# Second layer's experts: the first product as three products of 192 columns into one result

## The chip, the cores and the metric

The kernel runs on one core of a Trainium2 chip, as one program. A core has a matrix engine (TensorE, PE in the rows), a vector engine (VectorE, DVE), a scalar engine (ScalarE, ACT), GpSimd (POOL), and SyncE (SP), which issues most loads. TensorE's weight loads have rows of their own (PEld). The metric is the device time of one execution in microseconds, the median over several. Times within an execution come from one that was recorded by the hardware profiler.

## The reference

The model is two blocks, one after the other, each of two layers, on 256 tokens of width 1024. The change is in the expert part (`peer`) of the first block's second layer. Each token picks 16 of 16384 experts for each of 8 heads; an expert is a row u and a row v of two tables:

```
q = (xc @ wq).reshape(C, PEER_HEADS, 2, PEER_KEY_DIM)
...
top, pos = lax.top_k(cand, PEER_TOPK)
eidx = jnp.take_along_axis(cidx, pos, axis=-1)
g = jax.nn.softmax(top, axis=-1).astype(xc.dtype)
a = jax.nn.gelu(jnp.einsum('chkd,cd->chk', u_tab[eidx], xc))
return jnp.einsum('chk,chkd->cd', g * a, v_tab[eidx])
```

## The kernel before

Instead of gathering the rows of the picked experts for each token, the kernel computes most tokens densely: the 16384 experts are 128 blocks of 128, and for each block the first product multiplies the block's u rows with the tokens, gelu follows, the values are multiplied with a matrix of routing weights that is zero where an expert wasn't picked, and the second product multiplies with the block's v rows. In the second layer there are 256 tokens; `DENSE` gives 192 of them (TD = 192) to this dense way, and the other 64 go by gathers: an indirect DMA on GpSimd fetches rows (`gathered`, lines 892 to 909), and VectorE makes two passes of 1024 columns over each (line 895 takes the dot product, line 909 adds to a sum what the gather before it gave).

Float32 is multiplied as three products of two halves. `split` (lines 127 and 128) makes a high half on ScalarE and a low half on VectorE in a type that TensorE multiplies in one pass. `mm3` (lines 182 to 187) multiplies high by high (line 185), high by low (186) and low by high (187) and adds all three in one result bank; its first operand is the stationary one, which TensorE loads as weights. Weights come through `wload`: a DMA on SyncE's queue into `raw`, `split` into `whi` and `wlo`, four of each ahead.

`peer` (from line 697) calls `expert_in` for each block. Blocks 0 to 29 of the second layer take the branch `whole` ahead of the loop. The other 98 blocks run within the loop over c, in each round with: the first product of block c; gelu into `G` (line 868); the product with the routing weights into `A` (line 790); its split into `Ahl` (line 793, and line 795 for the last 64 tokens apart); up to one gather; and the second product of the block three rounds earlier (LAG = 3). The second product is six 512 wide products by `mm3` for 128 tokens and four of line 823 for the remaining 64.

The first product goes over the width of 1024 in eight slices of 128 (k). For TD = 192 the high and the low half of the tokens lie side by side in `h2`, so one product 384 wide (line 859) multiplies the high half of the weights with both at once: columns 0 to 191 of the bank get high by high, columns 192 to 383 high by low. A second product, 192 wide (line 858, or 861 in the first slice), adds low by high to columns 0 to 191. After the last slice ScalarE copies the right part out of the bank (line 864) and VectorE adds the left part to it (line 865), and gelu reads the sum.

The program is written in the order above, and a scheduler of the framework puts the instructions of each engine in an order of its own. Each engine works through its own in that order, and semaphores tie them together.

Of the kernel before, what the change touches and what calls it, by code (L numbers as in the profile page):

```python
# [9 lines left out]
F32 = mybir.dt.float32  # L10
# [33 lines left out]
def r3(ap, a):  # L44
    return ap.rearrange("p (a b) -> p a b", a=a)


class Net:
# [791 lines left out]

    def expert_in(self, lp, l, c, h2, h32, TD, whole):


        nc, mm = self.nc, self.nc.tensor.matmul
        ps = self.psum(True)
        src = ps[:, :TD]
        if whole:
            u = r3(self.wraw(self.i["peer_uT"][l, c]), 8)
            for k in range(8):
                mm(src, u[:, k], h32[:, k, :TD], start=k == 0, stop=k == 7)  # L850
        else:
            u = self.wload(self.i["peer_uT"][l, c], 8)
            for k in range(8):
                if TD > 192:
                    self.mm3(src, (u[0][:, k], u[1][:, k]), (h2[:, k, 0, :TD], h2[:, k, 1, :TD]), k == 0, k == 7)
                    continue
                if k:
                    mm(src, u[1][:, k], h2[:, k, 0, :TD], start=False, stop=False)  # L858
                self.last = mm(r3(ps[:, :2 * TD], 2), u[0][:, k], h2[:, k, :, :TD], start=k == 0, stop=k == 7).ins  # L859
                if k == 0:  # L860
                    mm(src, u[1][:, k], h2[:, k, 0, :TD], start=False, stop=False)
            if TD <= 192:
                both = lp.tile([128, TD], F32, tag="Gs", name="Gs", bufs=2)
                nc.scalar.copy(both, ps[:, TD:2 * TD])
                nc.vector.tensor_add(both, both, src)
                src = both
        g = lp.tile([128, TD], F32, tag="G", name="G", bufs=15 if TD > 256 else 36)
        nc.scalar.activation(g, src, AF.Gelu_apprx_tanh)
        return g
# [766 lines left out]
```

## Time and profile before

| what | us |
|---|---|
| median of 3 runs | 3451.87 |
| lowest and highest run | 3449.92, 3456.09 |
| the profiled execution | 3459.74 |
| span of its instructions | 3458.0 |
| TensorE busy in the span | 3322.4 (96%) |
| VectorE busy | 2624.0 (76%) |
| ScalarE busy | 1777.2 (51%) |

The span runs from the first to the last instruction of the profiled execution; its own time is 1.74 us longer. TensorE's products are pipelined: one starts before the one ahead of it has ended, so that their durations add up to more than the time that passes, and distances between starts say more.

### The profile page before, as it was taken

To read this page: it belongs to the slowest core of one execution; us is meant where nothing else is said; L and a number is where in the kernel's file an instruction comes from. 1 tells how busy PE (TensorE), PEld (TensorE's weight loads), DVE (VectorE), ACT (ScalarE), POOL (GpSimd) and SP (SyncE) were. 2 spreads that over 40 slices of the span, in tenths; PEclk is the share of its full clock that TensorE was granted. 3 is DMA by queue.
4 is the path that set the end of the run, shared out by engine and by line. 5 is a ranking of instruction groups with operands and counts; after the bars stand their busy time and mean duration, and the time that the engine had idled before them with its cause. 6 is when DMAs were issued, how large, how long until landed. Compare 5 with 4: busy or idle time off the path is not lost.

```text
span 3458.0 us, 53681 instructions
## 1 busy us (share of the span) xinstructions
PE 3322.4 (96%) x19573; PEld 2856.2 (83%) x19573; DVE 2624.0 (76%) x5467; ACT 1777.2 (51%) x3763; POOL 513.2 (15%) x434
## 2 busy tenths in 40 slices
PE   8999999899899999999999999989999989999998
PEld 5665788788888888888877988869999988889887
DVE  3533449988988888999966679599999957746764
ACT  3433332396444444444445545557777745545554
POOL 0000000112333333333300000122222100000000
PEclk9999999999999999999999999999999999999999
DMA  7555232457999999999944555799999843255332
GB/s 254 179 201 209 84 125 88 163 175 287 375 385 370 369 384 369 385 394 390 381 176 153 176 169 172 264 346 382 373 378 372 327 159 137 98 180 180 120 122 104
DMA packets 196456, 860.56 MB, mean 249 GB/s; under 512 B 23920, under 2 KB 25664, under 8 KB 159712
## 3 DMA queue, kind: packets, MB, share of 16 engines
q1 hardware_dynamic: 141840, 505.94, 40.4%
q0 software_dynamic: 54352, 351.20, 26.5%
q8 instruction: 154, 2.52, 0.3%
q14 instruction: 110, 0.90, 0.1%
HBM read 816.15 MB, written 40.89 MB: 248 GB/s over the span
## 4 chain that ended last, share of the span: by engine, by line
PE 54%; issue 24%; DVE 9%; DMA 7%; POOL 5%; ACT 1%; POOLq 0%; DVEq 0%; SPq 0%; ACTq 0%
PE pf L187 6%; PE pf L186 6%; PE pf L185 6%; PE ps L185 5%; PE ps L187 5%; PE ps L186 5%; PE pf L859 4%; POOL gat L892 3%; DMA gat<-peer_uv,idx 3%; PE ps L823 3%; DVE wlo L128 3%; PE pf L858 2%; DVE gacc L909 2%; PE pf L369 2%; PE ps L261 1%
## 5 line engine op out<-in xcount | busy, mean ns | idle before, releaser
L128 DVE TENSOR_TENSOR wlo<-raw,whi 128x1024 fp32r<-128x1024 f32 x778 | 940.9, 1221 | 386.4 <-ACT whi L127 381.5
L127 ACT CAST whi<-raw 128x1024 fp32r<-128x1024 f32 x778 | 814.4, 1047 | 574.4 <-PE pf L186 206.6
L892 POOL DMA_INDIRECT gat<-peer_uv,idx x256 | 403.9, 1578 | 926.0 <-DVE gacc L909 895.0
L187 PE MATMUL pf<-h2hl,wlo 128*128 128x320 f32 (+2 forms) x1152 | 373.2, 324 | 43.3 <-DVE wlo L128 43.1
L895 DVE SCALAR_TENSOR_TENSOR gat<-gat,h 128x1024 f32<-128x1024 f32 x256 | 311.9, 1219 | 77.4 <-DMA gat<-peer_uv,idx 77.1
L185 PE MATMUL pf<-h2hl,whi 128*128 128x320 f32 (+2 forms) x1152 | 370.3, 321 | 0.0
L186 PE MATMUL pf<-h2hl,whi 128*128 128x320 f32 (+2 forms) x1152 | 369.7, 321 | 0.0
L909 DVE SCALAR_TENSOR_TENSOR gacc<-gat,pga,gacc 128x1024 f32<-128x1024 f32 x253 | 323.4, 1278 | 0.0
L186 PE MATMUL ps<-wlo,Ahl 128*128 128x512 f32 x768 | 302.2, 393 | 7.0 <-DVE wlo L128 7.0
L185 PE MATMUL ps<-whi,Ahl 128*128 128x512 f32 x768 | 301.1, 396 | 2.5 <-ACT Ahl L127 2.5
L187 PE MATMUL ps<-whi,Ahl 128*128 128x512 f32 x768 | 301.3, 392 | 0.5 <-DVE Ahl L128 0.5
L187 PEld LDWEIGHTS pf<-h2hl,wlo 128*128 128x128 f32 x1152 | 223.3, 194 | 52.1 <-DVE wlo L128 49.4
L859 PE MATMUL pf<-h2hl,whi 128*128 128x384 f32 x784 | 238.9, 360 | 3.9 <-ACT whi L127 3.7
L185 PEld LDWEIGHTS pf<-h2hl,whi 128*128 128x128 f32 x1152 | 223.2, 194 | 7.4
L186 PEld LDWEIGHTS pf<-h2hl,whi 128*128 128x128 f32 x1152 | 222.6, 193 | 7.4
L127 ACT CAST Ahl<-A 128x320 fp32r<-128x320 f32 (+1 forms) x256 | 103.7, 405 | 220.7 <-DVE A L790 215.8
L1021 PE MATMUL ps<-o,og 128*128 128x128 f32 x1024 | 171.1, 297 | 6.0 <-ACT og L1020 4.8
L858 PE MATMUL pf<-h2hl,wlo 128*128 128x192 f32 x686 | 175.3, 256 | 0.0
L187 PEld LDWEIGHTS ps<-whi,Ahl 128*128 128x128 f32 x768 | 144.7, 188 | 33.5 <-DVE Ahl L128 1.0
L186 PEld LDWEIGHTS ps<-wlo,Ahl 128*128 128x128 f32 x768 | 144.6, 188 | 32.0 <-DVE wlo L128 9.7
L896 ACT ACTIVATE pga<-pga 128x1 f32<-128x1 f32 x256 | 51.4, 201 | 230.3 <-DVE gat L895 230.2
L185 PEld LDWEIGHTS ps<-whi,Ahl 128*128 128x128 f32 x768 | 144.8, 189 | 26.8 <-ACT Ahl L127 4.5
(591 smaller groups left out, 7749.4 us busy)
## 6 DMA issues: line engine op xcount, KB each, us to landing
raw<-peer_uT SPq DMA_DIRECT2D x256, 512.0 KB, 7.2
raw<-peer_v SPq DMA_DIRECT2D x256, 512.0 KB, 7.1
raw<-ada_w SPq DMA_DIRECT2D x96, 512.0 KB, 4.6
wd<-wb POOLq DMA_DIRECT2D x32, 1024.0 KB, 6.4
raw<-w_g SPq DMA_DIRECT2D x48, 512.0 KB, 3.8
win<-wd POOLq DMA_DIRECT2D x16, 1280.0 KB, 11.0
raw<-wq SPq DMA_DIRECT2D x32, 512.0 KB, 3.6
raw<-w2o SPq DMA_DIRECT2D x32, 512.0 KB, 3.2
```

The source lines that it names most:

```text
L127: nc.scalar.copy(hi, src)
L128: nc.vector.tensor_sub(lo, src, hi.bitcast(F32))
L185: mm(ps, ah, bh, start=start, stop=False)
L186: mm(ps, ah, bl, start=False, stop=False)
L187: self.last = mm(ps, al, bh, start=False, stop=stop).ins
L823: nc.tensor.matmul(acc[nd][n], ahl[:, 2 * TD - part:], v[e][:, n], start=b == 0 and e == 0, stop=b == 127 and e == 1)
L858: mm(src, u[1][:, k], h2[:, k, 0, :TD], start=False, stop=False)
L859: self.last = mm(r3(ps[:, :2 * TD], 2), u[0][:, k], h2[:, k, :, :TD], start=k == 0, stop=k == 7).ins
L892: nc.gpsimd.indirect_dma_start(out=uv.rearrange("p a b -> p (a b)"), out_offset=None, in_=i["peer_uv"], in_offset=bass.IndirectOffsetOnAxi ...
L895: nc.vector.scalar_tensor_tensor(uv[:, 0], uv[:, 0], 1.0, h2, op0=OP.mult, op1=OP.mult, accum_out=a[:, 0:1])
L909: self.nc.vector.scalar_tensor_tensor(acc, uv[:, 1], a[:, 1:2], acc, op0=OP.mult, op1=OP.add)
L1021: nc.tensor.matmul(ps[:, j * 128:j * 128 + 128], og[:, j], o1[:, jj], start=True, stop=True)
```

## The change

For TD = 192 the first product now goes through `mm3` as it does in the first layer: in each slice three products of 192 columns, high by high, high by low and low by high, all added in columns 0 to 191 of the bank. The copy on ScalarE, the addition on VectorE and their buffer `Gs` are gone; gelu reads the bank.

```
-                if TD > 192:
-                    self.mm3(src, (u[0][:, k], u[1][:, k]), (h2[:, k, 0, :TD], h2[:, k, 1, :TD]), k == 0, k == 7)
-                    continue
-                if k:
-                    mm(src, u[1][:, k], h2[:, k, 0, :TD], start=False, stop=False)
-                self.last = mm(r3(ps[:, :2 * TD], 2), u[0][:, k], h2[:, k, :, :TD], start=k == 0, stop=k == 7).ins
-                if k == 0:
-                    mm(src, u[1][:, k], h2[:, k, 0, :TD], start=False, stop=False)
-            if TD <= 192:
-                both = lp.tile([128, TD], F32, tag="Gs", name="Gs", bufs=2)
-                nc.scalar.copy(both, ps[:, TD:2 * TD])
-                nc.vector.tensor_add(both, both, src)
-                src = both
+                self.mm3(src, (u[0][:, k], u[1][:, k]), (h2[:, k, 0, :TD], h2[:, k, 1, :TD]), k == 0, k == 7)
```

In the following rows an instruction has its line, its operation, what it writes and reads, and its size; `pf` and `ps` are result banks, `u` comes as `whi` and `wlo`. Lines behind the edit have numbers lower by 13 in the changed kernel.

TensorE in a round of the loop, before, from the last instruction of a second product on into the first product of a block (its first two slices):

```order
L823 MATMUL ps<-wlo,Ahl 128x512
L859 MATMUL pf<-h2hl,whi 128x384
L861 MATMUL pf<-h2hl,wlo 128x192
L858 MATMUL pf<-h2hl,wlo 128x192
L859 MATMUL pf<-h2hl,whi 128x384
L858 MATMUL pf<-h2hl,wlo 128x192
```

The same place in the changed kernel, its first slice and the start of the second:

```order
L823 MATMUL ps<-wlo,Ahl 128x512
L185 MATMUL pf<-h2hl,whi 128x192
L186 MATMUL pf<-h2hl,whi 128x192
L187 MATMUL pf<-h2hl,wlo 128x192
L185 MATMUL pf<-h2hl,whi 128x192
```

Sixteen instructions of a first product have become 24; the alternation with the second product of another block is the same in both.

VectorE in a round with a gather, before (`gat` is the gathered row, `gacc` the sum, `wlo` the low half of weights):

```order
L790 TENSOR_TENSOR A<-G,win 128x192
L895 SCALAR_TENSOR_TENSOR gat,pga<-gat,h_21336 128x1024
L128 TENSOR_TENSOR Ahl<-A,Ahl 128x192
L909 SCALAR_TENSOR_TENSOR gacc<-gat,pga,gacc 128x1024
L128 TENSOR_TENSOR wlo<-raw,whi 128x1024
L865 TENSOR_TENSOR Gs<-Gs,pf 128x192
L128 TENSOR_TENSOR wlo<-raw,whi 128x1024
```

And in the changed kernel:

```order
L790 TENSOR_TENSOR A<-G,win 128x192
L882 SCALAR_TENSOR_TENSOR gat,pga<-gat,h_21336 128x1024
L896 SCALAR_TENSOR_TENSOR gacc<-gat,pga,gacc 128x1024
L128 TENSOR_TENSOR Ahl<-A,Ahl 128x192
L128 TENSOR_TENSOR wlo<-raw,whi 128x1024 x2
```

The addition into `Gs` is gone, and the low half of `Ahl` has moved behind the second pass of the gather.

TensorE at the end of the stage, before: behind the last second product come products of another part (line 315), and then the fold that joins dense and gathered tokens (lines 833 and 834):

```order
L823 MATMUL ps<-wlo,Ahl 128x512
L315 MATMUL pf<-raw 128x128 x13
L833 MATMUL ps<-gat,fold 128x512
L834 MATMUL ps<-gacc,fold 128x512
L833 MATMUL ps<-gat,fold 128x512
L834 MATMUL ps<-gacc,fold 128x512
L315 MATMUL pf<-raw 128x128 x3
```

And in the changed kernel:

```order
L823 MATMUL ps<-wlo,Ahl 128x512
L833 MATMUL ps<-gat,fold 128x512
L834 MATMUL ps<-gacc,fold 128x512
L833 MATMUL ps<-gat,fold 128x512
L834 MATMUL ps<-gacc,fold 128x512
L315 MATMUL pf<-raw 128x128 x16
```

The 13 products have moved behind the fold.

## Rows read from the trace of the kernel before

**Rows 1.** Spans and granted clock of the core.

```profile
core 0: 3458.0 us, clock 0.986
```

**Rows 2.** Instructions of line 859: durations (min/median/max), first and last start.

```profile
L859 PE MATMUL pf<-h2hl,whi x784: 333/361/575, 2301.7 to 2764.9; 128*128 128x384 f32 x196
```

**Rows 3.** Busy time by stretch: length, engines with instruction counts, clock, DMA share, GB/s.

```profile
2700.00:2750.00 50.00, 50.00 (x285) 45.48 (x285) 47.44 (x73) 35.97 (x79) 6.69 (x4) 1.00 0.90 354
...
2310.00:2765.00 455.00, 453.36 (x2559) 412.02 (x2560) 435.79 (x655) 322.97 (x697) 90.17 (x62) 1.00 0.93 366
```

**Rows 4.** Chain that ended last, 2410 to 2480: shares, then start, length, what.

```profile
by line: PE pf L859 33.6%; PE ps L823 21.1%; PE pf L858 13.9%; PE ps L187 10.0%; PE ps L186 9.9%; PE ps L185 9.9%; PE pf L861 1.9%
...
2410.18 0.92 PE ps L823 x4
...
2479.18 0.92 PE ps L823 x4
```

**Rows 5.** Who waited for whom, 2310 to 2765: us in total, times, longest.

```profile
PE pf L859 <- ACT whi L127: 3.7, 1, 3.7
...
PE pf L859 <- DVE Gs L865: 0.2, 1, 0.2
```

**Rows 6.** Timeline of TensorE, one block's first product: start, length, what.

```profile
2502.95 0.33 PE L859 MATMUL pf<-h2hl,whi 128*128 128x384 f32 x1
2503.12 0.25 PE L861 MATMUL pf<-h2hl,wlo 128*128 128x192 f32 x1
2503.20 0.28 PE L858 MATMUL pf<-h2hl,wlo 128*128 128x192 f32 x1
2503.32 0.36 PE L859 MATMUL pf<-h2hl,whi 128*128 128x384 f32 x1
2503.51 0.25 PE L858 MATMUL pf<-h2hl,wlo 128*128 128x192 f32 x1
2503.60 0.37 PE L859 MATMUL pf<-h2hl,whi 128*128 128x384 f32 x1
2503.80 0.25 PE L858 MATMUL pf<-h2hl,wlo 128*128 128x192 f32 x1
...
2505.25 0.39 PE L185 MATMUL ps<-whi,Ahl 128*128 128x512 f32 x1
```

**Rows 7.** Timeline of TensorE's weight loads in the same block.

```profile
2503.12 0.19 PEld L858 LDWEIGHTS pf<-h2hl,wlo 128*128 128x128 f32 x1
2503.23 0.19 PEld L859 LDWEIGHTS pf<-h2hl,whi 128*128 128x128 f32 x1
2503.34 0.19 PEld L858 LDWEIGHTS pf<-h2hl,wlo 128*128 128x128 f32 x1
2503.51 0.19 PEld L859 LDWEIGHTS pf<-h2hl,whi 128*128 128x128 f32 x1
```

**Rows 8.** Timeline of line 1374, products 64 wide, and of its loads.

```profile
2912.12 1.95 PE L1374 MATMUL ps<-xs,dec 128*128 128x64 f32 x16
...
2912.07 1.86 PEld L1374 LDWEIGHTS ps<-xs,dec 128*128 128x128 f32 x16
...
L1374 PE MATMUL ps<-xs,dec x128: 275/275/323, 2912.1 to 3288.3; 128*128 128x64 f32 x128
```

**Rows 9.** Timeline of 256 wide products in the second layer's queries.

```profile
2059.56 0.28 PE L186 MATMUL pf<-h2hl,whi 128*128 128x256 f32 x1
...
2060.39 0.28 PE L187 MATMUL pf<-h2hl,wlo 128*128 128x256 f32 x1
```

**Rows 10.** Groups by line, 2310 to 2765: count, busy us, mean ns, idle before.

```profile
L865 DVE TENSOR_TENSOR Gs<-Gs,pf 128x192 f32<-128x192 f32 x97 | 33.6, 347 | 0.0
L864 ACT COPY Gs<-pf 128x192 f32<-128x192 f32 x97 | 30.5, 314 | 16.4 <-PE pf L859 13.6
```

**Rows 11.** Chain that ended last, behind the stage.

```profile
2778.11 2.90 PE pf L315 x26
```

**Rows 12.** Groups by line, whole span: loads of high halves in lines 185, 186.

```profile
L185 PEld LDWEIGHTS pf<-h2hl,whi 128*128 128x128 f32 x1152 | 223.2, 194 | 7.4
L186 PEld LDWEIGHTS pf<-h2hl,whi 128*128 128x128 f32 x1152 | 222.6, 193 | 7.4
```

## The prediction

> **What bounds the kernel now.** The execution spans 3458.0 us at a granted TensorE clock of 0.986 of full speed [rows 1]. The edit touches one stage only, and its own line finds it: the 384 wide products of line 859 run from 2301.7 to 2764.9 us, 784 of them [rows 2], which is 98 blocks by 8 slices. So the next view to read is the busy time of that stretch [rows 3]: TensorE is busy 453.36 of 455 us, VectorE 435.79, ScalarE 322.97, and the DMA engines stand at 0.93. Three resources are nearly full, so the shares alone don't say which one paces. The chain of waits does: in 70 us from the middle of the stage it names TensorE lines and nothing else, and the group of four closing products of a block returns every 4.60 us (2410.18 to 2479.18 is 69.00 us for 15 blocks) [rows 4]. The list of who waited for whom agrees: in the whole stage TensorE's products waited once for ScalarE, 3.7 us, and once for VectorE, 0.2 us [rows 5]. TensorE bounds the stage. Every nanosecond added to a block there comes out at the end, and relief on VectorE or ScalarE is worth nothing.
>
> **What a block costs on TensorE now.** The durations of single products overlap, so I go by the distances between starts [rows 6]. The first product of a block runs from 2502.95 to 2505.25, where the first of the 512 wide products starts: 2.30 us for 16 instructions. The other 2.30 us of 4.60 are ten 512 wide products, which the edit leaves alone. Within a slice there are about 0.09 us from a 192 wide product to the next one (2503.51 to 2503.60) and 0.20 us from a 384 wide one (2503.60 to 2503.80), together 0.29.
>
> **The change part by part.** Columns first: a slice streamed 384 + 192 = 576 columns and will stream 3 x 192 = 576. Columns neither gain nor lose anything. What is added is one product per slice, and with it one weight load: 24 of each per block instead of 16.
>
> The added load decides. At the start of a block the trace has several loads in a row with only 192 wide products between them, and these start at 2503.12, 2503.23, 2503.34: 0.11 us apart [rows 7], though a product of 192 columns needs only 0.08 to 0.09 (2503.12 to 2503.20). The products follow their loads: from the one at 2503.20 to the next it is 0.12 us, not 0.09 [rows 6]. In the rest of the block each 192 wide product alternates with a 384 wide one, which gives the loads time. A second place shows the same for a still narrower product: 16 products of 64 columns with full 128 x 128 float32 weights take 1.95 us, the last one's 0.275 among it, so (1.95 - 0.275)/15 = 0.112 us each, and their 16 loads (1.86 - 0.19)/15 = 0.111 us each [rows 8]. A third of the width, and the same distance: it isn't the columns. I read 0.108 to 0.112 us as the least distance of two loads of such weights. After the change every product is 192 wide, so every one waits for its load.
>
> The Trainium skill's page "TensorE: Matmul & The Clock Gate", section "LDWEIGHTS (loading the stationary operand)", gives a load as its columns divided by 1.2 per ns, so 107 ns for 128 columns, whatever matmul stands behind it. The rows above agree within a few ns; by the page alone a block's first product would be 24 x 107 ns = 2.57 us and the loss about 26 us (an estimate).
>
> By the rows, the first product of a block becomes 24 x 0.110 = 2.64 us against 2.30: plus 0.34 us. Lower bound within this case: 0.108, and the second product of a block, whose load starts early, 0.02 sooner: 2.57, plus 0.27. Upper bound: 0.112, so 2.69, plus 0.39. From above there is a further row: 256 wide products of the same kind, back to back, stand (2060.39 - 2059.56)/7 = 0.119 us apart [rows 9], and 192 wide ones should not be slower: 24 x 0.119 = 2.86, plus 0.56. From below, if the loads hide fully: 24 x 0.088 = 2.11, minus 0.19. I take 0.110, since rows 7 are these very weights at this very width.
>
> How many blocks pay: the first of the 98 waits for its weights [rows 5], the others for TensorE alone. 97 x 0.34 = **33 us**.
>
> What goes: ScalarE's copy of 128 x 192 out of the result (0.314 us) and VectorE's addition (0.347 us), once a block each [rows 10]. Neither is on the chain. VectorE's 435.79 us over 455/4.60 = 99 blocks are 4.40 us per block and fall to 4.06, while a block grows to 4.94: VectorE, 0.2 us from pacing the stage before, ends 0.9 us behind. The gelu reads the result directly, and its value is used three blocks later, so an earlier or later gelu costs nothing. VectorE's order within a block shifts: the low half of A now comes behind both passes of a gather. The accumulating pass takes the gather before, so it adds no wait, and three blocks of lead (15 us) hide the later low half; I cost it at nothing. Without that lead one pass more would stand ahead of the second kind of product in each block that has a gather. The DMA engines move the same bytes, 0.93 x 4.60 = 4.3 us per block, at a lower density. Behind the stage, 13 products that stood ahead of the final fold move behind it; 26 such instructions take 2.90 us [rows 11], so at most 1.5 us less before the fold, or as much later. I take nothing.
>
> **Sum.** The profiled execution took 3459.74 us, 7.87 above the median of the runs shown, 3451.87. With 33 us it would be 3492.7; against the median it is 3451.87 + 33 = **3484.9 us**, 1% slower.
>
> **The rivals.**
> *The loads hide: faster.* If a load can start under two products, all of them follow each other at 0.088 us, as those behind a 192 wide one do now; a block is 2.11 + 2.30 = 4.41 us, VectorE (4.06) and the DMA engines (4.3) still fit under it, and the stage gains 97 x 0.19 = 18 us: 3433 us. For it speak the distances of 0.08 and 0.09 in rows 6. Against it: each of those has a load that started under a longer product or right after one, and where three loads follow each other they are 0.11 apart [rows 7]. The two sides meet at 2.30/24 = 0.096 us per product. The Trainium skill's same page, section "Back-to-back issue gap", speaks for this side: it has 81 ns per matmul at 128 columns and 131 at 512 in a stream of loads and matmuls, so about 89 at 192 (an estimate), which would make some 3436 us. Here ten 512 wide products take 2.30 us, 230 ns each, so its figures don't fit this trace, and I give them little.
> *The load isn't added.* The first two products of a slice use the same weights. Were the second load left out, a slice had two loads (0.22 us) under 3 x 0.088 = 0.26 us, and 3433 us again. Against it: in the first layer's blocks the same helper makes the same pair of products, and both of its lines have 1152 loads [rows 12].
> *Slower still.* If what holds the 256 wide products at 0.119 is the load with something around it, and not their columns, a block costs 2.86 + 2.30 us: 97 x 0.56 = 54 us, 3506 us. The starts in rows 7 speak against it.
> *No difference.* That takes 0.093 to 0.099 us per product, within 0.2% (6.9 us) of 3451.87. No row shows such a distance.
>
> **How the numbers follow.** The load-paced case, 0.105 to 0.114 us, has 0.76; the 256 wide distance and beyond, 0.08; loads partly hidden, 0.099 to 0.105 and still slower, 0.05; no difference 0.03; the gain in both forms 0.08. A measurement of this kernel can tell about 0.2% from no change, so slower has 0.89, same 0.03, faster 0.08. The load-paced case with its bounds (26 to 38 us) and the spread of the runs shown (2 below, 4 above) is 3476 to 3494. To take in the case above it and a part of the partly hidden one, the range goes from 3472 to 3505.
>
> **What would show it.** The closing group of a block should return every 4.9 to 5.0 us, the loads of a block should start 0.11 us apart all through, TensorE should still be the whole chain of the stage, and VectorE's share there should fall from 96% to about 82%. Products 0.09 apart would prove the first rival, 0.12 the third. If the block takes 4.94 us and the total grows by much less than 33 us, the step from block to end failed and the time was made up behind the stage. Waits of TensorE for VectorE would say that the shifted order there was not free.

## The result, and the profile after

The changed kernel takes 3486.82 us in the median of 4 runs (3483.08 to 3492.55), the kernel before 3450.89 in 4. The ratio is 1.0106 with a 95% interval of 1.0089 to 1.0124: slower, by 35.9 us, where 33 were forecast.

The chain of waits in the same 70 us as [rows 4], changed kernel (shares of the stretch by line, then start, length, what):

```profile
by line: PE ps L823 18.4%; PE pf L187 18.2%; PE pf L186 18.0%; PE pf L185 17.5%; PE ps L185 9.7%; PE ps L186 9.3%; PE ps L187 9.2%
...
2412.70 0.91 PE ps L823 x4
...
2477.48 0.92 PE ps L823 x4
```

It names nothing but TensorE again, and the closing group returns 13 times in 64.78 us: 4.98 us a block instead of 4.60.

The busy time of the whole stage, which is now longer, answers [rows 3]:

```profile
2310.00:2800.00 490.00, 487.96 (x3321) 445.37 (x3320) 406.94 (x551) 292.30 (x594) 104.89 (x65) 1.00 0.88 337
```

TensorE is as full as before, 487.96 of 490 us. VectorE falls from 96% to 83%, the DMA engines from 0.93 to 0.88.

The timeline of TensorE in one block answers [rows 6]:

```profile
2503.15 0.25 PE L185 MATMUL pf<-h2hl,whi 128*128 128x192 f32 x1
2503.23 0.28 PE L186 MATMUL pf<-h2hl,whi 128*128 128x192 f32 x1
2503.35 0.28 PE L187 MATMUL pf<-h2hl,wlo 128*128 128x192 f32 x1
2503.46 0.27 PE L185 MATMUL pf<-h2hl,whi 128*128 128x192 f32 x1
...
2505.69 0.27 PE L187 MATMUL pf<-h2hl,wlo 128*128 128x192 f32 x1
2505.80 0.42 PE L185 MATMUL ps<-whi,Ahl 128*128 128x512 f32 x1
2506.07 0.40 PE L186 MATMUL ps<-wlo,Ahl 128*128 128x512 f32 x1
```

Only the first distance is 0.08; from there the products stand 0.11 to 0.12 apart, and the first product of the block lasts 2505.80 - 2503.15 = 2.65 us against 2.30. The first 512 wide product behind it takes 0.27 us to its successor, not the 0.23 of the other nine. The weight loads of the same block answer [rows 7]:

```profile
2503.15 0.19 PEld L186 LDWEIGHTS pf<-h2hl,whi 128*128 128x128 f32 x1
2503.26 0.19 PEld L187 LDWEIGHTS pf<-h2hl,wlo 128*128 128x128 f32 x1
2503.37 0.19 PEld L185 LDWEIGHTS pf<-h2hl,whi 128*128 128x128 f32 x1
...
2505.72 0.19 PEld L185 LDWEIGHTS ps<-whi,Ahl 128*128 128x128 f32 x1
```

They start 0.11 us apart from one end of the block to the other; the last row is the load of the first 512 wide product.

**Where the time went.** The two profiled executions differ by only 23.3 us of span (3458.0 and 3481.3), less than the medians. The last products of the branch `whole` and the last second product bound the stage. They read, before (line 850) and after (line 849), then line 823 before and after, with the first and last start in the second pair of numbers:

```profile
L850 PE MATMUL pf<-h2f,raw x480: 326/326/687, 2076.2 to 2235.5; 128*128 128x192 f32 x160
```

```profile
L849 PE MATMUL pf<-h2f,raw x480: 326/326/658, 2067.2 to 2221.4; 128*128 128x192 f32 x160
```

```profile
L823 PE MATMUL ps<-whi,Ahl x384: 387/392/628, 832.0 to 2777.5; 128*128 128x512 f32 x192
```

```profile
L823 PE MATMUL ps<-whi,Ahl x384: 387/392/398, 830.4 to 2803.0; 128*128 128x512 f32 x192
```

The stage took 2777.5 - 2235.5 = 542.0 us before and 2803.0 - 2221.4 = 581.6 after, 39.6 us more. The recorded execution of the changed kernel reached the stage 14.1 us sooner. Up to there every engine's instructions are the same in the same order, and in the traces of the experiments below this point lies anywhere from 2216 to 2236 us, so this is the difference between two executions and no effect of the change. Behind the stage 680.5 us became 678.3, 2.2 less; in the experiments' traces that part takes 675 to 690, so 2 us there tell nothing. Without the 14.1, that is 37.4 us, close to the 35.9 of the medians.

### The profile page after: what moved, and what is told of

It reads as the page before. It is cut to its first block, busy times and chain, and to the rows that moved or that the text cites. A ratio compares the mean times of both kernels' runs of the same rounds, so it can differ in the third digit from the quotient of the medians.

```text
span 3481.3 us, 55056 instructions
## 1 busy us (share of the span) xinstructions
PE 3354.5 (96%) x20357; PEld 2890.3 (83%) x20357; DVE 2598.1 (75%) x5369; ACT 1747.6 (50%) x3665; POOL 526.3 (15%) x434
## 4 chain that ended last, share of the span: by engine, by line
PE 51%; issue 26%; DVE 9%; DMA 7%; POOL 5%; ACT 2%; POOLq 0%; DVEq 0%; SPq 0%; ACTq 0%
PE pf L187 8%; PE pf L186 8%; PE pf L185 8%; PE ps L185 4%; PE ps L187 4%; PE ps L186 4%; DMA gat<-peer_uv,idx 4%; POOL gat L879 4%; PE ps L823 3%; DVE wlo L128 3%; DVE gacc L896 2%; PE ps L1008 1%; PE pf L369 1%; DMA raw<-peer_v 1%; PE ps L261 1%
## 5 line engine op out<-in xcount | busy, mean ns | idle before, releaser
L187 PE MATMUL pf<-h2hl,wlo 128*128 128x320 f32 (+3 forms) x1936 | 588.4, 304 | 36.6 <-DVE wlo L128 36.2
L185 PE MATMUL pf<-h2hl,whi 128*128 128x320 f32 (+3 forms) x1936 | 583.1, 301 | 4.5 <-ACT whi L127 4.5
L186 PE MATMUL pf<-h2hl,whi 128*128 128x320 f32 (+3 forms) x1936 | 584.0, 302 | 0.0
L879 POOL DMA_INDIRECT gat<-peer_uv,idx x256 | 416.8, 1628 | 938.4 <-DVE gacc L896 597.7
L187 PEld LDWEIGHTS pf<-h2hl,wlo 128*128 128x128 f32 x1936 | 373.7, 193 | 45.2 <-DVE wlo L128 42.3
L185 PEld LDWEIGHTS pf<-h2hl,whi 128*128 128x128 f32 x1936 | 373.2, 193 | 16.7 <-ACT whi L127 5.3
L186 PEld LDWEIGHTS pf<-h2hl,whi 128*128 128x128 f32 x1936 | 373.0, 193 | 11.5
L1008 PEld LDWEIGHTS ps<-o,og 128*128 128x128 f32 x1024 | 137.7, 191 | 33.9 <-ACT og L1007 22.0
L1007 ACT ACTIVATE og<-o,eT 128x128 f32<-128x128 bf16 x320 | 147.6, 527 | 4.6 <-DVE o L999 4.6
```

What stands on the lines that cost most here:

```text
L185: mm(ps, ah, bh, start=start, stop=False)
L186: mm(ps, ah, bl, start=False, stop=False)
L187: self.last = mm(ps, al, bh, start=False, stop=stop).ins
L879: nc.gpsimd.indirect_dma_start(out=uv.rearrange("p a b -> p (a b)"), out_offset=None, in_=i["peer_uv"], in_offset=bass.IndirectOffsetOnAxi ...
L1007: nc.scalar.activation(og[:, j], o2[:, :, jj], AF.Copy, scale=eT[:, 1, t0 + j:t0 + j + 1])
L1008: nc.tensor.matmul(ps[:, j * 128:j * 128 + 128], og[:, j], o1[:, jj], start=True, stop=True)
```

## The experiments

Ten kernels, in three sets, each set on one chip with runs of the kernel before: median 3457.10 there in the first, 3454.74 in the second, 3455.74 in the third. Totals of single runs are read with care, since runs of one kernel spread over some 15 us; the time of a block in the chain is steady to 0.01 us and decides. Diffs are against the kernel named.

**1. High by low into columns of its own.** The kernel before, with three products per slice; copy and addition stay.

```
-                if k:
-                    mm(src, u[1][:, k], h2[:, k, 0, :TD], start=False, stop=False)
-                self.last = mm(r3(ps[:, :2 * TD], 2), u[0][:, k], h2[:, k, :, :TD], start=k == 0, stop=k == 7).ins
...
+                mm(src, u[0][:, k], h2[:, k, 0, :TD], start=k == 0, stop=False)
+                mm(ps[:, TD:2 * TD], u[0][:, k], h2[:, k, 1, :TD], start=False, stop=False)
+                self.last = mm(src, u[1][:, k], h2[:, k, 0, :TD], start=False, stop=k == 7).ins
```

> Three products of 192 columns a slice as in the changed kernel, but high by low goes to columns 192 to 383 of the bank and the copy and the addition stay. Load theory (a 128 column load of these weights can start no sooner than 0.11 us after the one before it, and every 192 wide product waits for its own): a block of 4.98 us, as in the changed kernel, some 3487 us. Rival (three products that add to the same columns one after the other hold each other up): the second product is free of it, so the block falls well under 4.98, to about 4.7 or less.

Measured: 3489.65 us in one run. The chain of waits of this kernel:

```profile
2422.70 0.92 PE ps L823 x4
...
2442.65 0.92 PE ps L823 x4
```

Those are four blocks in 19.95 us, 4.99 us each. So it isn't the adding into the same columns, and the price comes whole with the split into three products: with the copy and the addition still there the block costs what it costs without them. (Single blocks at other places take longer, so that the stage as a whole takes some 10 us more than in the changed kernel; why isn't settled.)

**2. Fewer columns under the same loads.** The changed kernel with both corrections cut to 64 tokens.

```
-                self.mm3(src, (u[0][:, k], u[1][:, k]), (h2[:, k, 0, :TD], h2[:, k, 1, :TD]), k == 0, k == 7)
...
+                hh = [(src, u[0][:, k], h2[:, k, 0, :TD])]
+                cut = [(ps[:, :64], u[n][:, k], h2[:, k, 1 - n, :64]) for n in range(2)]
+                ops = cut + hh if k else hh + cut
+                for n, (o, a, b) in enumerate(ops):
+                    self.last = mm(o, a, b, start=k == 0 and n == 0, stop=k == 7 and n == 2).ins
```

> Changed kernel, with high by low and low by high cut to the first 64 of 192 tokens (the corrections of the other 128 tokens are left out), so that a slice streams 320 columns instead of 576 under the same three loads. Load theory: nothing changes, a block stays at 4.98 us. Rival (columns pace the products): 8 slices x 256 columns x 0.45 ns = 0.9 us less, a block of some 4.1 us, where VectorE (4.06) begins to pace.

Measured: 3495.32 us in one run. The chain, in which a block's first product is one row:

```profile
2436.21 2.65 PE pf L860 x24
...
2476.10 2.65 PE pf L860 x24
```

Eight blocks in 39.89 us, 4.99 us, and 2.65 us for the 24 products, though they stream 320 columns a slice and not 576. Columns don't pace these products.

**3. Half the load.** As before, with 64 columns of weights in place of 64 tokens.

```
-                cut = [(ps[:, :64], u[n][:, k], h2[:, k, 1 - n, :64]) for n in range(2)]
+                cut = [(ps[:64, :TD], u[n][:, k, :64], h2[:, k, 1 - n, :TD]) for n in range(2)]
```

> Changed kernel, with high by low and low by high made with 64 of the 128 weight columns (the corrections of half of the experts are left out); 24 products of 192 columns stay. Load theory: if a load's time goes with its columns, the loads of a slice take 0.11 + 0.055 + 0.055 = 0.22 us, under the 3 x 0.088 = 0.26 us of its products; a block of 4.4 to 4.5 us. Rival (a fixed price per product of 0.11 us whatever it loads): a block stays at 4.98 us.

Measured: 3457.14 us in one run, level with the kernel before. Chain, and the timeline of TensorE's loads in one block:

```profile
2426.89 2.29 PE pf L860 x24
...
2463.69 2.29 PE pf L860 x24
```

```profile
2500.42 0.14 PEld L860 LDWEIGHTS pf<-h2hl,wlo 128*64 128x64 f32 x1
2500.51 0.14 PEld L860 LDWEIGHTS pf<-h2hl,whi 128*64 128x64 f32 x1
```

Eight blocks in 36.80 us, 4.60. The fixed price per product is out: 24 products of 192 columns now take 2.29 us, and a load of half the columns lasts 0.14 us, not 0.19, and the next one starts 0.09 us after it. But the block didn't come down to the 4.4 to 4.5 expected. I had added up the loads of a slice and laid them under the sum of its products. The measured slice is 2.29/8 = 0.286 us, and the distances from start to start within it are 0.088, 0.088 and 0.11: the one product of three whose successor has a full load still costs that load. Loads don't make up for each other. In these rows one load goes with one product, and each pair costs the longer of the two.

**4. The products of the kernel before, grouped.**

```
-                if k:
-                    mm(src, u[1][:, k], h2[:, k, 0, :TD], start=False, stop=False)
-                self.last = mm(r3(ps[:, :2 * TD], 2), u[0][:, k], h2[:, k, :, :TD], start=k == 0, stop=k == 7).ins
-                if k == 0:
-                    mm(src, u[1][:, k], h2[:, k, 0, :TD], start=False, stop=False)
...
+                for k in range(8):
+                    mm(r3(ps[:, :2 * TD], 2), u[0][:, k], h2[:, k, :, :TD], start=k == 0, stop=False)
+                for k in range(8):
+                    self.last = mm(src, u[1][:, k], h2[:, k, 0, :TD], start=False, stop=k == 7).ins
```

> Kernel before, its 16 products in another order: first the eight of 384 columns, then the eight of 192. Load theory with the price put where the two traces now put it (a 192 wide product costs the load of its successor, 0.11 to 0.12 us, a 384 wide one its columns, 0.172): 8 x 0.172 + 8 x 0.112 + 0.03 = 2.30 us, a block stays at 4.60 us and the total at 3451. Rival (as the prediction put it, the long neighbour gives time to the loads of the short one: alternating 0.09 and 0.20, 192 wide ones among themselves 0.11): 8 x 0.20 + 8 x 0.11 = 2.48 us, a block of 4.78 us, 17 us slower, 3468.

Measured: 3505.11 us in the median of 4 runs, ratio 1.0139 (1.012 to 1.0159). TensorE's timeline and the chain of this kernel:

```profile
2502.36 1.57 PE L858 MATMUL pf<-h2hl,whi 128*128 128x384 f32 x8
2503.77 1.03 PE L860 MATMUL pf<-h2hl,wlo 128*128 128x192 f32 x8
2504.64 0.42 PE L185 MATMUL ps<-whi,Ahl 128*128 128x512 f32 x1
```

```profile
by line: DVE wlo L128 36.8%; DVE gacc L907 14.0%; issue 13.0%; DVE gat L893 9.6%; ACT whi L127 8.7%; DVE Ahl L128 6.1%; DVE Gs L863 5.2%; ACT G L866 3.9%; DVE A L790 3.6%; DVEq L128 0.6%
```

On TensorE the theory holds: the first product takes 2504.64 - 2502.36 = 2.28 us, as against 2.30 alternating; the first 512 wide product behind it takes 0.25 us where it took 0.23, so that the two orders cost the same. Eight 192 wide products cost (1.03 - 0.25)/7 = 0.111 each and eight 384 wide ones (1.57 - 0.36)/7 = 0.173. So the price belongs to the 192 wide product, whatever its neighbour. The total went another way, which neither theory had: TensorE doesn't pace this kernel. The scheduler put the gelu on ScalarE right behind the copy, and there it waits for VectorE's addition, 146.7 us in 78 waits between 2350 and 2750 where it was 46.9 in 46 in the same stretch before; VectorE waits for the gelu in turn, and the chain runs through VectorE. Experiments 9 and 10 take that exchange away.

**5. Grouped, with short loads.** As 4, with low by high in bfloat16.

```
+            if src.tensor.name == "peer_uT" and src.offset >= NE * D:
+                lo = lo.bitcast(BF)[:, :1024]
...
+                self.h2b = pa.tile([128, 8, TD], BF, name="h2b")
+                nc.gpsimd.tensor_copy(self.h2b, h2[:, :, 0, :TD].bitcast(F32))
...
+                    self.last = mm(src, u[1][:, k], self.h2b[:, k], start=False, stop=k == 7).ins
```

> Kernel before with its products grouped (eight of 384 columns, then eight of 192), and low by high made in bfloat16: VectorE writes the low half of these weights as bfloat16, and the tokens' high half is copied to bfloat16 once. Load theory with a load of bfloat16 weights that is much shorter than 0.11 us: the 192 wide products fall to 0.088 us, 8 x 0.173 + 8 x 0.088 + 0.03 = 2.12 us, TensorE's part of a block 4.42 us; VectorE (4.40 busy per block) is then level with it, so a block of 4.45 to 4.6 us and a total of 3437 to 3451. Rival (every product has a fixed price of 0.11 us): TensorE's part stays at 4.60 us and the total at 3451 or, if VectorE's order is worse, above.

Measured: 3506.70 us in the median of 4 runs, ratio 1.0151 (1.0128 to 1.0175). TensorE in one block:

```profile
2504.47 0.83 PE L865 MATMUL pf<-h2b,wlo 128*128 128x192 bf16 x8
2505.09 0.48 PE L187 MATMUL ps<-whi,Ahl 128*128 128x512 f32 x1
2505.40 0.39 PE L188 MATMUL ps<-wlo,Ahl 128*128 128x512 f32 x1
```

TensorE's share of the expectation came: eight 192 wide products with bfloat16 weights stand (0.83 - 0.25)/7 = 0.083 us apart, 0.25 being one product's own row, where they stood 0.111 apart. From the first of them to the 512 wide product it is 0.62 us, and that one then takes 0.31 us instead of 0.23; together the eight cost 0.62 + 0.08 = 0.70 us, 0.088 each, as expected. The block didn't follow, for from 2420 to 2480 us 58% of the chain is waiting for loads from memory (38.0% second weights, 19.6% first), with the DMA engines at 0.85 to 0.91 in three windows of 50 us. The forecast of the total is a miss: a faster TensorE doesn't help where other engines and loads pace the stage. Why these loads come late isn't shown.

**6. The relief alone.** The kernel before without the copy and the addition.

```
-            if TD <= 192:
-                both = lp.tile([128, TD], F32, tag="Gs", name="Gs", bufs=2)
-                nc.scalar.copy(both, ps[:, TD:2 * TD])
-                nc.vector.tensor_add(both, both, src)
-                src = both
```

> Kernel before without the copy on ScalarE and the addition on VectorE (high by low is left out of the result, its columns are still computed). Prediction's theory (TensorE alone paces the stage, the relief is worth nothing): a block stays at 4.60 us and the total within 0.2% of before. Rival (the exchange between ScalarE and VectorE holds the stage now and then, and the change got part of its price back by removing it): some us faster, at most 0.35 us x 97 = 34 us.

Measured: 3458.90 us in the median of 10 runs, ratio 1.0011 (0.9998 to 1.0024). The chain of waits from 2420 to 2480 us:

```profile
by line: PE pf L859 34.0%; PE ps L823 20.4%; PE pf L858 14.1%; PE ps L186 10.0%; PE ps L185 10.0%; PE ps L187 9.8%; PE pf L861 1.9%
...
2423.90 0.92 PE ps L823 x4
2428.50 0.92 PE ps L823 x4
```

It is TensorE's alone, and a block takes 4.60 us. The relief of VectorE and ScalarE is worth nothing in that order of the work.

**7. The third load short, in the changed kernel.**

```
-                self.mm3(src, (u[0][:, k], u[1][:, k]), (h2[:, k, 0, :TD], h2[:, k, 1, :TD]), k == 0, k == 7)
...
+                for k in range(8):
+                    mm(src, u[0][:, k], h2[:, k, 0, :TD], start=k == 0, stop=False)
+                    mm(src, u[0][:, k], h2[:, k, 1, :TD], start=False, stop=False)
+                for k in range(8):
+                    self.last = mm(src, u[1][:, k], self.h2b[:, k], start=False, stop=k == 7).ins
```

> Changed kernel (three products of 192 columns into one result), with low by high in bfloat16 and moved behind the other sixteen. Load theory: 16 x 0.111 + 8 x 0.088 + 0.03 = 2.51 us instead of 2.68, a block of 4.81 us, 16 us less than the changed kernel, some 3470 us. Rival (a fixed price per product): a block stays at 4.98 us, 3487.

Measured: 3464.45 us in one run, and the chain and the eight short products of a block:

```profile
2427.97 0.92 PE ps L828 x4
...
2475.64 0.92 PE ps L828 x4
```

```profile
2501.99 0.83 PE L866 MATMUL pf<-h2b,wlo 128*128 128x192 bf16 x8
2502.60 0.48 PE L187 MATMUL ps<-whi,Ahl 128*128 128x512 f32 x1
2502.92 0.40 PE L188 MATMUL ps<-wlo,Ahl 128*128 128x512 f32 x1
```

The load of that first 512 wide product:

```profile
2502.58 0.19 PEld L187 LDWEIGHTS ps<-whi,Ahl 128*128 128x128 f32 x1
```

Ten blocks in 47.67 us, 4.77 instead of 4.98, with nothing left out and TensorE pacing: 24 products as in the changed kernel, and a third of them (0.83 - 0.25)/7 = 0.083 us apart instead of 0.111. Their loads are short (0.10 us a row, not 0.19), but their type has changed as well, so this run alone doesn't tell the one from the other; experiment 3 does. The 0.61 us to the 512 wide product aren't their whole price: its load starts only 0.02 us ahead of it, and it takes 0.32 us instead of 0.23.

**8. Two short loads of three.** The changed kernel's one result, both corrections in bfloat16, and a second cast of the weights on ScalarE.

```
+                both = lo.bitcast(BF)
+                self.split(raw, hi, both[:, :1024])
+                nc.scalar.copy(both[:, 1024:], raw)
...
+                for k in range(8):
+                    mm(src, u[0][:, k], h2[:, k, 0, :TD], start=k == 0, stop=False)
+                for k in range(16):
+                    self.last = mm(src, u[1][:, k], self.h2b[:, k % 8, k // 8], start=False, stop=k == 15).ins
```

> Changed kernel's one result, with both corrections in bfloat16: eight products of 192 columns high by high, then sixteen in bfloat16; ScalarE casts the weights once more (1.05 us per block), there is no copy and no addition. By the distances now measured: 8 x 0.111 + 16 x 0.077 + 0.08 = 2.20 us, a block of 4.50 us against 4.60 before, 97 x 0.10 = 10 us faster than before: some 3441. Rival (the added cast on ScalarE and the new order of its instructions pace the stage, as VectorE and the loads did in the grouped version with short loads): a block of 4.7 us or more, slower than before.

Measured: 3464.82 us in the median of 12 runs, ratio 1.0026 (1.0016 to 1.0037): 0.8% under the changed kernel's 1.0106, and still slower than before. The forecast of 3441 is a miss. TensorE has its short block:

```profile
2502.69 1.03 PE L867 MATMUL pf<-h2hl,whi 128*128 128x192 f32 x8
2503.57 1.49 PE L869 MATMUL pf<-h2b,wlo 128*128 128x192 bf16 x16
2504.84 0.48 PE L191 MATMUL ps<-whi,Ahl 128*128 128x512 f32 x1
```

That is 2504.84 - 2502.69 = 2.15 us for 24 products, less than the 2.30 before. Part of that comes back in the first 512 wide product, which takes 0.32 us (2504.84 to 2505.16) instead of 0.23, so TensorE saves 0.06 us a block and not 0.15; the 0.077 us of the expectation was an eighth of 0.61 to 0.62 us, and the products stand 0.083 apart. The second product now waits at times for the low half of its weights from VectorE, the chain has VectorE, ScalarE and loads in it, and the stage takes 553 us where it took 542. No version here that computes the whole result beats the kernel before.

**9 and 10. Grouped, without the exchange.** Versions 4 and 5 without the copy and the addition, as in 6.

> The grouped version (eight products of 384 columns, then eight of 192) without the copy and the addition (high by low is left out of the result). If the exchange of copy, addition and gelu between ScalarE and VectorE made the grouped version slow: TensorE paces again, a block of 4.58 us, the total level with before. Rival (grouping itself frees the weights' buffers later and makes the loads late): it stays near 3505.

> Grouped version with low by high in bfloat16, without the copy and the addition (high by low is left out of the result). If only the exchange stood in its way: TensorE's part of 4.42 us shows, unless the DMA engines (4.3 us per block) pace it first: a block of 4.4 to 4.5 us, 3432 to 3443. Rival (loads from memory come late whatever the exchange does): above 3460.

Measured: 3471.60 and 3433.01 us, one run each. The second one's chain, 2600 to 2700:

```profile
by line: PE pf L863 31.3%; PE ps L828 21.0%; PE pf L865 15.3%; PE ps L187 11.3%; PE ps L189 10.7%; PE ps L188 10.5%
...
2602.69 1.42 PE pf L863 x8
...
2638.05 1.42 PE pf L863 x8
```

Eight blocks in 35.36 us, 4.42 us: with short loads and without the exchange TensorE paces there and shows its whole part, as expected. Earlier in the same run loads from memory pace at times, with the DMA engines at 0.97 to 0.99 in four windows of 50 us between 2350 and 2650: there is little room left in them behind TensorE. Version 9 is half a hit. It lies 34 us under version 4, so the copy, the addition and the waits for them were most of what made that one slow (the addition's own 0.35 us a block would be 34 us by itself; no run separates that work from the waits), but 16 us over the kernel before: a late load of weights (8.2 to 9.5 us in the chain) and VectorE's low halves hold TensorE now and then. Why the scheduler's order comes out worse there isn't settled.

## Why the prediction was right

**TensorE bounds the stage, and what it gains or loses arrives at the end.** Right, and shown from three sides: the change adds 0.38 us a block and the stage grows by 39.6 us; experiment 6 takes the relief alone and changes nothing that shows; experiment 1 keeps copy and addition and pays the full price.

**Columns neither gain nor lose, the added load decides.** Right. With 320 columns instead of 576 the block stays at 4.99 us (2); with two loads of three halved it returns to 4.60 (3); with a third of the products in bfloat16, whose loads are short, it falls to 4.77 (7). The rival in which the loads hide and the one in which the load isn't added are out by the loads' own rows, 0.11 us apart throughout. So is the one that is slower still: 0.111, not 0.119.

**The size.** 0.34 us per block was forecast, 0.38 came. Two terms were a little small: the distance is 0.111 and not 0.110, so the first product takes 2.65 us and not 2.64, and the first 512 wide product behind it takes 0.27 us and not 0.23, since its own load starts late as well: at 2505.72, 0.08 us ahead of it, where before it started at 2505.08, 0.17 ahead. The working had let the price end with the last 192 wide product. 97 x 0.383 = 37 us.

**How the price was read.** The sentence that the 384 wide product "gives the loads time" explained the alternating 0.09 and 0.20 us wrongly. Grouped, the same sixteen products cost no more (4), so a 192 wide product pays 0.111 us beside a long one as well. In [rows 6] the 384 wide product's start seems to stand where its predecessor's columns end, about 0.03 us before its weights can be there, and its own time seems longer by that: 0.20 instead of 0.173. No row marks when weights are in place, but the loads' rows agree at three places: from the start of a product's own load it is one load (0.11 us) and the time of its columns (0.173 us for 384, 0.23 for 512) to the start of the next product. For the 384 wide product of [rows 7] that is 2503.51 + 0.11 + 0.173 = 2503.79, and the next one starts at 2503.80. For the first 512 wide product of the changed kernel it is 2505.72 + 0.11 + 0.23 = 2506.06, measured 2506.07; for that of experiment 7 2502.58 + 0.11 + 0.23 = 2502.92, measured 2502.92. With it the change is counted at once: per slice, two products of 0.111 replace one of 0.173, 8 x 0.049 = 0.39 us.

**What goes.** Right for this order of the work. VectorE fell to 83% where 82 was forecast, its new order cost TensorE nothing that shows (two waits of 1.5 and 0.5 us at the end of the stage, where the kernel before has two of 1.0 and 0.5). What the fold's new place is worth doesn't show: the part behind the stage took 2.2 us less, within its spread from run to run. Not seen was how narrow the cover is: with the same instructions in another order the exchange between ScalarE and VectorE paces the stage (4).

## What to carry to other kernels

Count weight loads, not only columns: a product of the type used here that takes less time than the load behind it costs the load, so fusing two narrow products that share their weights into one wide product saves a load even if it needs an addition afterwards, as long as the addition has an engine with time. Look for the price in the distance between starts in the trace, at a place where several narrow products stand in a row. And before moving work on TensorE in a stage where three engines are nearly full, look at what order the scheduler then gives the others: that moved the total more than the products did.

## What the runs showed of the hardware

In the stage before and after the change, a load of 128 columns of float32-type weights holds the next load for 0.108 to 0.112 us. Products of 192 columns in a row with such loads stand 0.111 us apart, and 0.088 apart with loads of 64 columns (3). Products of 192 columns in bfloat16 stand 0.083 us apart (5, 7, 8), a little less than the 0.088 of the float32 type at the same width: not only the load is shorter. And a late load shows on the long product behind a row of narrow ones, too: its row takes 0.27 us instead of 0.23 behind float32-type products and 0.31 to 0.32 behind bfloat16 ones, so a row of narrow products is priced with the product behind it.
